# Three key pieces instead of four in a retention scan, and five changes of order, in a hybrid encoder block

## The chip, the core and the metric

The kernel runs on one core of one Trainium2 chip. The metric is device time in microseconds (us) of one execution. The engines are named as in the profile: PE (TensorE, matmuls) with PEld (its weight loads), DVE (VectorE), ACT (ScalarE), POOL (GpSimd) and SP (SyncE, which here only issues DMAs).

## The reference

One encoder block over 16 learned meta tokens and 1024 positions, width 1024. From one normed input `u` and one wide projection come two branches, which are gated and merged:

```
u = rms_norm(h); z = u @ w_in                     # rq rk rv rg | aq ak av ag | gr ga
# branch A, retention: 4 heads, keys of 128, values of 256, chunks of 128, forward and backward
s     = (q k^T) * decay;  inner = s v             # inside a chunk
kv    = (k * k_decay)^T v                         # a chunk's contribution
state = chunk_decay * state + kv                  # scanned over the chunks
o_r   = inner + (q * q_decay) @ state_prev        # both directions are added
o_r   = group_norm(o_r) * ret_nw * silu(rg);  y_r = o_r @ w_rb
# branch B, windowed attention: 8 heads in 2 groups, +-128 positions, meta keys, sink logit
p     = softmax(rotary(aq) rotary(ak)^T * scale + band)
o_a   = (p @ av) * silu(ag);  y_a = o_a @ w_ab
out   = (sigmoid(gr) * y_r + sigmoid(ga) * y_a) @ w_out
return (h + rms_norm(out))[meta tokens dropped]
```

The queries and keys of both branches are rotated (rotary positions) before use.

## The kernel before

Every float32 product is made of three matmuls (`mm3`): each operand is split into a high part (a cast, on ACT or POOL) and a low part (the rest, `dve_lo` on DVE), and high·high, low·high and high·low are added up in a PSUM bank. So each operand of TensorE comes from a cast on one engine and a subtraction on DVE.

The work goes through these stages, on one timeline without gaps:

1. *Head 0's queries and keys* (about 0 to 28 us), while the input arrives. `outs` holds one PSUM bank for each piece of columns; `evac_qk0` rotates the pieces later, three DVE operations and a POOL addition each.
2. *The retention* of four heads (to about 325 us). `retention(h, fill, begin)` scans the chunks c = 0..8 forward (`stage1`: value projection, transposed keys, scores; `stage2`: outputs and state), then c = 8..1 backward, where it normalizes and stores. In the backward loop it calls `fill(n)`, which takes n steps from a generator of other work: `gen_qk(h + 1)`, which projects the next head's keys and queries, then some steps of `pre` (partial products of the gates). A step is one `mm3`, so a piece of columns has KT = 8 steps whatever its width. `KEYS` does not exist here: keys are projected in the four `PIECES` (272, 256, 256 and 256 columns), queries in the two `HALVES` (512 each). `rope_late` rotates a projected piece: two DVE products out of PSUM, and then two accumulating DMAs from POOL's queue, which add the swapped halves. The keys of a head lie in a tile of four parts of 272 columns, `kt`; `ksl(c)` picks a chunk's 128 columns. At the end of the backward scan `begin` starts the next head: its value weights are loaded and split, high part on POOL, low part on DVE.
3. *The attention* (about 330 to 550 us). `gen_av` projects the values; `stage1` (scores `ps`, softmax in `raw`, `p` and `den`), `stage2` (transposes `pt`, their high parts `pah`, `pbh` and low parts `pal`, `pbl`) and `stage3` (`po`) run over 32 chunks, with `fill` in between, its shares in `FILL`. `hooked` counts the filling steps and calls what `BEGUN` lists for a step: `split_q` (high part `aqh`, low part `aql` of rotated queries), `keys(g, i)` (high part `kTh`, low part `kTl` of piece i of the keys of group g), `half_w`, `sum_fetch` and others.
4. *The phases z, r, a and o* (about 545 us to the end): gates, the two branch projections and the output projection, each by seven products per unit instead of eight (`Phase`, `PROD`). `prepare` builds and splits the left operands (`lhz`/`llz` in phase z, `lla` in phase a, `llo` in phase o) up to `LEAD` = 6 products ahead, and leaves the low part that it made last in `ahead[0]`. `refill` loads and splits the right operands of the next phase (`big<-...`, `T<-...`), spread over the products of the phase that runs. Units 0 and 1 of phase z are `early`: they make the sum S4 in three DVE operations at once.

The program's order on each engine is laid out by a planner with a simulated timeline (line 1706), from the order in which the code asks for things and from what it expects each to wait for. `tc.issue_after(i)`, and `follow(...)`, which enters several of them, let an instruction be laid out only after instruction i. Each engine then works through its own list in order.

Of the kernel before, what the change touches and what calls it, by code (L numbers as in the profile page):

```python
# [10 lines left out]
ALU = mybir.AluOpType  # L11
# [8 lines left out]
NH = 4  # L20
EPS = 1e-6
SCALE = 128 ** -0.5
PIECES = [(0, 272), (272, 528), (528, 784), (784, 1040)]
HALVES = [(16, 528), (528, 1040)]
MW = 416
# [14 lines left out]
def block_kernel(ctx: ExitStack, tc: tile.TileContext, x0, xT, x, meta, w_in, w_rb, w_ab, w_out, post_w,  # L40
# [136 lines left out]
    cr = ra.tile([P, T], F32, name="cr")  # L177
    sr = ra.tile([P, T], F32, name="sr")

    held = []  # L180
    BEHIND = "aq1_10", "aq3_10"

    def rope_late(t, a, b, o, nm):

        n = b - a
        m = ra.tile([P, 512], F32, tag="m", bufs=4, name=f"m_{nm}")
        nc.vector.tensor_tensor(m[:, 0:n], t[:, 0:n], sr[:, a:b], ALU.mult)
        nc.vector.tensor_tensor(o[:, 0:n], t[:, 0:n], cr[:, a:b], ALU.mult)

        def rotate():  # L190
            for r in (0, 64):
                nc.gpsimd.dma_start(o[64 - r:128 - r, 0:n], m[r:r + 64, 0:n], accum_op=ALU.add)
        if nm in BEHIND:
            held.append(rotate)
        else:
            rotate()

    def rope_evac(t, a, b, o, nm):
        n = b - a
        m1, m2 = (ra.tile([P, 512], F32, tag="m", bufs=4, name=f"m{i}_{nm}") for i in (1, 2))  # L200
        nc.vector.tensor_tensor(m1[:, 0:n], t[:, 0:n], cr[:, a:b], ALU.mult)
        nc.vector.tensor_tensor(m2[64:128, 0:n], t[0:64, 0:n], sr[0:64, a:b], ALU.mult)
        rot = nc.vector.tensor_tensor(m2[0:64, 0:n], t[64:128, 0:n], sr[64:128, a:b], ALU.mult).ins
        nc.gpsimd.tensor_tensor(o[:, 0:n], m1[:, 0:n], m2[:, 0:n], ALU.add)
        return rot


# [53 lines left out]
    def evac_qk0(*pieces):  # L261
        if 0 not in qk:
            qk[0] = [], ra.tile([P, 4, 272], F32, tag="kp", bufs=2, name="kr0")
        q, kt = qk[0]
        for i in pieces:
            m0, a, b, t = (outs[2:] + outs[:2])[i]
            if m0:
                o = kt[:, i]
            else:
                o = ra.tile([P, 512], F32, tag="q", bufs=6, name=f"qr0_{i}")  # L270
                q.append(o)
            rot = rope_evac(t, a, b, o, f"qk0_{i}")
        return rot

    with tc.tile_pool(name="setup", bufs=1, reuse_waits="tile") as st:
# [46 lines left out]
            nc.tensor.matmul(idle[:, 0:KT * (32 + NM)], zeros[:, 0:P], zeros, start=True, stop=True)  # L322


        outs = [(P, a, b, t(f"pk0_{a}")) for (a, b), t in zip(PIECES, (pj, pj, p1, p3))]
        outs = [(0, a, b, p2(f"pq0_{a}")) for a, b in HALVES] + outs

        def qk0_mm(k):
# [53 lines left out]
        first = [projT(wv0, 0, "pv0_0", vmeta0), projT(wv0, 1, "pv0_1"), projT(wv0, 2, "pv0_2")]  # L382
    ra.tile([P, 32], F32, name="space_q")
    with tc.issue_after(rotated):
        turned = evac_qk0(4)
    with tc.issue_after(turned):
        nc.vector.memset(ms, 1.0)
        nc.vector.tensor_scalar(ms[0:NM, 0:1], sumsq[0:NM, 0:1], 1.0 / D, EPS, op0=ALU.mult, op1=ALU.add)
# [61 lines left out]
    def gen_qk(h):  # L450
        w = load_w(w_in, U_QK + h)
        q, kt = [], ra.tile([P, 4, 272], F32, tag="kp", bufs=2, name=f"kr{h}")
        qk[h] = (q, kt)
        for i, (a, b) in enumerate(PIECES):
            t = yield from proj(w, P, a, b, f"pk{h}_{i}")
            rope_late(t, a, b, kt[:, i], f"k{h}_{i}")
            yield
        for i, (a, b) in enumerate(HALVES):
            t = yield from proj(w, 0, a, b, f"pq{h}_{i}")
            o = ra.tile([P, 512], F32, tag="q", bufs=6, name=f"qr{h}_{i}")  # L460
            rope_late(t, a, b, o, f"q{h}_{i}")
            q.append(o)
            yield
# [3 lines left out]
    def retention(h, fill, begin=lambda: None):  # L467
# [147 lines left out]
        for c in range(NB, 0, -1):  # L615
            o = op[c - 1]
            if c > 1:
                nxt = kvb[c - 1]
                if c < NB:
                    nxt = rp.tile([P, 256], F32, tag="S", bufs=2, name=f"Sb{h}_{c}")  # L620
                    nc.vector.scalar_tensor_tensor(nxt, state["b"], cdb(h), kvb[c - 1], op0=ALU.mult, op1=ALU.add)
                state["b"] = nxt
                state["bs", c - 1] = split_state(nxt, f"b{h}_{c}")
            if c < NB:
                bh, bl = state["bs", c]
                pb = p3(f"pb{h}_{c}")
                last["pb"] = mm3(pb[:, 0:256], qs(qh, c), qs(ql, c), bh, bl, True, True)
                nc.vector.scalar_tensor_tensor(o, pb[:, 0:256], qdb(h, c), o, op0=ALU.mult, op1=ALU.add)
            bs = rp.tile([P, 6], F32, tag="bs", bufs=2, name=f"bs{h}_{c}")
            mv = rp.tile([P, 2], F32, tag="mv", bufs=2, name=f"mv{h}_{c}")  # L630
            rs = rp.tile([P, 1], F32, tag="rs", bufs=2, name=f"rs{h}_{c}")
            nc.vector.bn_stats(bs, o)
            nc.vector.bn_aggr(mv, bs)
            near = nc.vector.tensor_scalar(rs, mv[:, 1:2], EPS, None, op0=ALU.add).ins
            nc.gpsimd.tensor_tensor(rs, rs, mhalf[:, 0:1], ALU.pow)
            state["n", c] = lambda o=o, mv=mv, rs=rs: nc.vector.tensor_scalar(o, o, mv[:, 0:1], rs, op0=ALU.subtract,
                                                                              op1=ALU.mult)
            if c < NB:
                with tc.issue_after(near):
                    state["n", c + 1]()  # L640
            if c < 8:
                with ExitStack() as behind:
                    for p in pins:
                        behind.enter_context(tc.issue_after(p))
                    fill(KT)
            if c == 1:
                begin()
            if c < NB - 1:
                finish(c + 2)
# [20 lines left out]
    def split_q(hp, e_, i):  # L670
# [4 lines left out]
            if len(aqs) == 1:  # L675
                aw.tile([P, 48], F32, name="space_aq")
        h, l = (t.rearrange("p (t e q) -> p t e q", e=2, q=64)[:, :, e_] for t in aqs[hp, i][0])
        nc.scalar.copy(h, o)
        dve_lo(l, o, h)
        aqs[hp, i][1].add(e_)  # L680


    def fetch_aq(hp):
# [47 lines left out]
    def gen_ak(g, pieces_=range(4)):  # L731
        if not wak:
            wak.append(load_w(w_in, U_AK))
        for i in pieces_:
            a, b = PIECES[i]
            t = yield from proj(wak[0], P * g, a, b, f"pak{g}_{i}")
            o = rotated_k[g, i] = ra.tile([P, 272], F32, tag="ak", bufs=2, name=f"akr{g}_{i}")
            rope_late(t, a, b, o, f"ak{g}_{i}")
            if not g and i:
                keys(g, i - 1)  # L740
            yield
# [133 lines left out]
    with tc.issue_after(normed):  # L875
        evac_qk0(2)
        decay_table((0,))
        evac_qk0(3, 5)
    heads, drains = [], []

    def begin_head(h):
# [21 lines left out]
    def gen_av():  # L903
        w = load_w(w_in, U_AV)
        for c in range(9):
            mt = None if c else vmt
            t = projT(w, c, f"pav{c}", mt)
            if c == 0:
# [5 lines left out]
                for r in range(2):  # L914
                    nc.sync.dma_start(vm[32 * r + NM:32 * r + 2 * NM].bitcast(F32), mt)
            else:
                nc.scalar.activation(vah[:, c - 1], t[:, 0:256], AF.Copy, scale=rcol[:, c:c + 1])
                nc.vector.scalar_tensor_tensor(low_value(c - 1), t[:, 0:256], rcol[:, c:c + 1],
                                               vah[:, c - 1].bitcast(F32), op0=ALU.mult, op1=ALU.subtract)
# [46 lines left out]
    class Phase:  # L966
# [24 lines left out]
        def prepare(self, u, p):  # L991
# [30 lines left out]
                    g(t, self.block(u, "A12"), t, sub)  # L1022
            elif u in self.early:
                t = lp.tile([P, 4, P], F32, tag="st", bufs=3, name=f"st{self.nm}{u}S4")
                g(t, self.block(u, "A21"), self.block(u, "A22"), add)
                g(t, t, self.block(u, "A11"), sub)
                g(t, self.block(u, "A12"), t, sub)
                self.split(u, 3, t)
# [125 lines left out]
    def refill(nm, src):  # L1154
# [24 lines left out]
            for k, j in enumerate(n):  # L1179
                at.setdefault(j, []).append(lambda k=k: f(k))  # L1180

        if nm == "a":
            at = {-16: [load(0, 0)], -14: [load(1, 1)]}
            each(at, -13, split("B11", 0, 0))
            at.update({-11: [got("T1")], -10: [load(1, 0)], -9: [got("T2")], -5: [got("T3")], -1: [got("T4")]})
            each(at, -7, split("B21", 1, 0))
            each(at, -3, split("B22", 1, 1))
            return at

        first = -21 if nm == "z" else -17  # L1190
        at = {first: [load(0, 0), load(0, 1)], -13: [load(1, 1)], -9: [load(1, 0, range(3))]}
        def behind(f):
            def g(k):
                with tc.issue_after(ahead[0]):
                    f(k)
            return g

        step(at, range(first + 2, first + 6), behind(minus((0, 1), (0, 1), (0, 0))))
        step(at, (-13, -12, -11, -10), split("B11", 0, 0))
        step(at, (-11, -10, -9, -8), split("T1", 0, 1))  # L1200
# [209 lines left out]
    def attention():  # L1410
# [123 lines left out]
                 gen_aq(3, 0), gen_aq(3, 1), pre]  # L1534
        fill = filler([hooked(works, BEGUN)])[0]

        with follow(*latest):
            fill(3)
        with follow(*latest):
            stage1(0, 0)  # L1540
        for k, (hp, n) in enumerate(chunks):
# [28 lines left out]
            if k in (12, 14, 21):  # L1570
# [13 lines left out]
             76: [(sum_row, 3, 1)], 79: [(sum_fetch, 4)], 82: [(split_q, 2, 0, 0)], 88: [(sum_row, 4, 0)],  # L1584
             89: [(sum_row, 4, 1)], 90: [(split_q, 2, 1, 0)], 92: [(sum_fetch, 5)], 100: [(sum_row, 5, 0)],
             101: [(sum_row, 5, 1)], 102: [(fetch_aq, 3)], 104: [(keys, 1, 1)], 105: [(sum_fetch, 6)],
             110: [(split_q, 2, 0, 1)], 116: [(keys, 1, 2)], 117: [(half_w, 'q', 3, 0)], 121: [(half_w, 'q', 3, 1)],
             122: [(pre_fetch, 9)], 123: [(sum_row, 6, 0)], 124: [(sum_row, 6, 1)], 126: [(split_q, 2, 1, 1)],
             127: [(sum_fetch, 7)], 133: [(pre_sum, 9, 0)], 134: [(pre_sum, 9, 1)], 136: [(keys, 1, 3)],
             139: [(pre_sum, 9, 2)], 140: [(pre_parts, 9)], 141: [(pre_fetch, 10)], 145: [(split_q, 3, 0, 0)],  # L1590
             146: [(sum_row, 7, 0)], 147: [(sum_row, 7, 1)], 150: [(split_q, 3, 1, 0)], 152: [(pre_sum, 10, 0)],
             153: [(pre_sum, 10, 1)], 155: [(pre_sum, 10, 2)], 157: [(pre_parts, 10)], 158: [(pre_fetch, 11)],
             164: [(split_q, 3, 0, 1)], 166: [(pre_sum, 11, 0)], 167: [(pre_sum, 11, 1)], 168: [(pre_sum, 11, 2)],
             170: [(pre_parts, 11)], 171: [(pre_fetch, 12)], 172: [(split_q, 3, 1, 1)], 176: [(pre_sum, 12, 0)],
             178: [(pre_sum, 12, 1)], 179: [(pre_sum, 12, 2)], 181: [(pre_parts, 12)], 182: [(pre_fetch, 13)],
             187: [(pre_sum, 13, 0)], 188: [(pre_sum, 13, 1)], 189: [(pre_sum, 13, 2)], 190: [(pre_parts, 13)]}

# [112 lines left out]
```

## Time and profile before

| | us |
|---|---|
| median of 3 timed runs | 1034.35 |
| lowest and highest | 1034.12, 1037.31 |
| the profiled execution, whole | 1035.83 |
| the profiled execution, its span | 1034.1 |

| engine | busy us | share of the span | instructions |
|---|---|---|---|
| PE | 1022.3 | 99% | 5883 |
| PEld | 898.8 | 87% | 5883 |
| DVE | 831.9 | 80% | 1802 |
| ACT | 502.0 | 49% | 1129 |
| POOL | 226.3 | 22% | 368 |

A span runs from the first to the last instruction of the profiled execution; the execution's own time is 1.73 us longer. In rows of the timeline the columns are start and duration in us, engine, line of the code, operation, what it writes `<-` what it reads (buffer numbers left out), shape, count, and in brackets the engine's idle time just before and what ended it. Rows of the view of waits give who waited for what, the total in us, how often, and the longest.

### The profile page before, as it was taken

The numbers are of one execution on the slowest core, as the hardware profiler recorded it, in microseconds if no ns is written. First come the engines' busy times: TensorE is split into PE (matmuls) and PEld (weight loads), VectorE is DVE, ScalarE is ACT, GpSimd is POOL, SyncE is SP. The second block draws the span as 40 slices with busy tenths as digits, with TensorE's granted clock in tenths as the row PEclk, the third lists the DMA queues.
The fourth block names the chain that finished last, engine by engine and source line by source line (L and its number), as shares of the span: only waits on it lengthen the run. The fifth ranks groups of instructions, "written<-read, shape, count | busy, mean of one in ns | idle before, by whom it ended". The sixth has DMA issues, their size and how long they took to land. (4 is left out here: it accounts for less than half of the span.)

```text
span 1034.1 us, 17322 instructions
## 1 busy us (share of the span) xinstructions
PE 1022.3 (99%) x5883; PEld 898.8 (87%) x5883; DVE 831.9 (80%) x1802; ACT 502.0 (49%) x1129; POOL 226.3 (22%) x368
## 2 busy tenths in 40 slices
PE   9999999999999999999999999999999999999997
PEld 8998999989989888988888888888888888887886
DVE  7886759758876787777769999998989899777765
ACT  5531432523423466655667555455567456333442
POOL 3445244243341424443310000000000000110032
PEclk9999999999999999999999999999999999999999
DMA  9433123243241447666559589899874756889563
GB/s 360 164 87 88 63 46 87 76 78 112 80 97 62 103 152 206 184 183 174 154 171 347 178 287 330 312 319 319 276 265 141 257 196 200 246 216 330 139 122 81
DMA packets 98840, 188.45 MB, mean 182 GB/s; under 512 B 13024, under 2 KB 37632, under 8 KB 98192
## 3 DMA queue, kind: packets, MB, share of 16 engines
q1 hardware_dynamic: 81200, 162.89, 46.6%
q0 software_dynamic: 10176, 14.73, 9.5%
q10 hardware_dynamic: 7376, 9.73, 2.8%
q8 instruction: 46, 0.75, 0.3%
q14 instruction: 42, 0.34, 0.1%
HBM read 124.32 MB, written 57.68 MB: 176 GB/s over the span
## 5 line engine op out<-in xcount | busy, mean ns | idle before, releaser
L1310 POOL DMA_DIRECT2D mx_d<-c1a x4 | 3.6, 891 | 395.3 <-DMA a<-in_w_out_dram 368.6
L77 PE MATMUL bz<-big,llz 128*128 128x512 f32 x192 | 74.9, 390 | 0.5 <-DVE llz L92 0.5
L78 PE MATMUL bz<-big,lhz 128*128 128x512 f32 x192 | 74.4, 389 | 0.0
L76 PE MATMUL bz<-big,lhz 128*128 128x512 f32 x192 | 74.1, 389 | 0.0
L76 PE MATMUL pv<-wh,big 128*128 128x256 f32 x256 | 72.9, 285 | 0.0
L77 PE MATMUL pv<-wh,big 128*128 128x256 f32 x256 | 72.8, 284 | 0.0
L78 PE MATMUL pv<-wl,big 128*128 128x256 f32 x256 | 72.7, 284 | 0.0
L78 PE MATMUL bz<-T,lhz 128*128 128x512 f32 x176 | 68.5, 389 | 0.0
L77 PE MATMUL bz<-T,llz 128*128 128x512 f32 x176 | 68.5, 389 | 0.0
L76 PE MATMUL bz<-T,lhz 128*128 128x512 f32 x176 | 68.2, 389 | 0.0
L1450 ACT ACTIVATE p<-raw,nm 128x337 f32<-128x337 f32 (+1 forms) x64 | 35.5, 557 | 34.1 <-DVE nm L1447 30.5
L76 PE MATMUL paq<-big,wh 128*128 128x512 f32 x128 | 51.6, 403 | 0.0
L1463 POOL TENSOR_SCALAR p<-p,den 128x336 f32<-128x336 f32 (+2 forms) x60 | 32.6, 565 | 85.9 <-DVE den L1454 81.1
L78 PE MATMUL paq<-big,wh 128*128 128x512 f32 x128 | 50.2, 392 | 0.0
L77 PE MATMUL paq<-big,wl 128*128 128x512 f32 x128 | 50.2, 392 | 0.0
L76 PEld LDWEIGHTS pv<-wh,big 128*128 128x128 f32 x256 | 48.4, 189 | 0.4
L77 PEld LDWEIGHTS pv<-wh,big 128*128 128x128 f32 x256 | 48.3, 189 | 0.4
L78 PEld LDWEIGHTS pv<-wl,big 128*128 128x128 f32 x256 | 48.3, 189 | 0.3
L92 DVE TENSOR_TENSOR wl<-wr,wh 128x1024 fp32r<-128x1024 f32 x28 | 35.1, 1258 | 11.3 <-POOL wh L89 6.7
L77 PEld LDWEIGHTS bz<-big,llz 128*128 128x128 f32 x192 | 36.1, 188 | 8.1 <-DVE llz L92 0.8
L78 PEld LDWEIGHTS bz<-big,lhz 128*128 128x128 f32 x192 | 36.0, 188 | 7.5
L76 PEld LDWEIGHTS bz<-big,lhz 128*128 128x128 f32 x192 | 36.1, 188 | 7.5
(621 smaller groups left out, 3591.2 us busy)
## 6 DMA issues: line engine op xcount, KB each, us to landing
wrz<-in_w_in_dram SPq DMA_DIRECT2D x32, 512.0 KB, 6.0
wr<-in_w_in_dram SPq DMA_DIRECT2D x29, 512.0 KB, 4.0
we<-in_w_in_dram SPq DMA_DIRECT2D x16, 512.0 KB, 4.2
tg<-tg_d SPq DMA_DIRECT2D x32, 256.0 KB, 5.3
e<-e ACTq DMA_DIRECT2D x20, 256.0 KB, 2.4
e<-e SPq DMA_DIRECT2D x20, 256.0 KB, 4.6
xn<-in_x_dram SPq DMA_DIRECT2D x8, 512.0 KB, 9.4
oTr_d<-ost SPq DMA_DIRECT2D x16, 256.0 KB, 2.1
```

What stands on the lines that cost most here:

```text
L76: nc.tensor.matmul(o, ah, bh, start=first, stop=False, **kw)
L77: nc.tensor.matmul(o, al, bh, start=False, stop=False, **kw)
L78: latest[:] = [nc.tensor.matmul(o, ah, bl, start=False, stop=last, **kw).ins]
L92: return nc.vector.tensor_tensor(o, i, hi.bitcast(F32), ALU.subtract).ins
L1310: nc.gpsimd.dma_start(d, to, accum_op=ALU.add)
L1450: last["exp"] = nc.scalar.activation(pp[:, x_, w0 - o:w0 - o + 1 + wid], r[:, 0:1 + wid], AF.Exp, scale=-1.0, bias=nm_[:, x_:x_ + 1], accu ...
L1463: nc.gpsimd.tensor_scalar(v, v, den[:, x_:x_ + 1], 1.0, op0=ALU.mult, op1=ALU.mult)
```

## The change

The retention's keys are projected in three pieces, `KEYS`, of 272, 256 and 512 columns. The last one is written through a view of two parts of 256 columns in `kt` (`key_piece`, and `like` for the operands beside it). The shares in the backward scans of heads 0 to 2 become 9, 5, 6, 6, 6, 8, 8 steps for c = 1..7, 48 in all, instead of 8 each; for head 3 they stay at 8. Head 0's pieces are evacuated accordingly, one fewer, and the last key piece takes the bank of tag `p3`.

Five changes of order stand beside that:

- `gen_av` stops once more after the last value projection and before its evacuation; the attention first splits both queries of pair 0 and lays that evacuation out behind their casts (`split_q` returns its cast for that);
- `keys(1, 2)` moves from filling step 116 to 120;
- `split_q(3, 1, 1)` moves from filling step 172 to 169;
- the first sum of S4 of the early units is laid out behind `ahead[0]`;
- in `refill`, the splits of the output projection's right operands (phase "a") are laid out behind `ahead[0]`, as those of other phases were.

```diff
+KEYS = [(0, 272), (272, 528), (528, 1040)]
 PIECES = [(0, 272), (272, 528), (528, 784), (784, 1040)]
...
+    def key_piece(t, i, n):
+        return t[:, 2:4, 0:256] if i == 2 else t[:, i, 0:n]
+
+    def like(t, o):
+        return t.rearrange("p (a c) -> p a c", a=2) if len(o.shape) > 2 else t
...
-        nc.vector.tensor_tensor(o[:, 0:n], t[:, 0:n], cr[:, a:b], ALU.mult)
+        nc.vector.tensor_tensor(o, like(t[:, 0:n], o), like(cr[:, a:b], o), ALU.mult)
...
-                nc.gpsimd.dma_start(o[64 - r:128 - r, 0:n], m[r:r + 64, 0:n], accum_op=ALU.add)
+                nc.gpsimd.dma_start(o[64 - r:128 - r], like(m[r:r + 64, 0:n], o), accum_op=ALU.add)
...
-        outs = [(P, a, b, t(f"pk0_{a}")) for (a, b), t in zip(PIECES, (pj, pj, p1, p3))]
+        outs = [(P, a, b, t(f"pk0_{a}")) for (a, b), t in zip(KEYS, (pj, p1, p3))]
...
-        turned = evac_qk0(4)
+        turned = evac_qk0(3)
...
-        for i, (a, b) in enumerate(PIECES):
+        for i, (a, b) in enumerate(KEYS):
             t = yield from proj(w, P, a, b, f"pk{h}_{i}")
-            rope_late(t, a, b, kt[:, i], f"k{h}_{i}")
+            rope_late(t, a, b, key_piece(kt, i, b - a), f"k{h}_{i}")
...
-                    fill(KT)
+                    fill(KT if h == NH - 1 else (9, 5, 6, 6, 6, 8, 8)[c - 1])
...
-        nc.scalar.copy(h, o)
+        upper = nc.scalar.copy(h, o).ins
         dve_lo(l, o, h)
         aqs[hp, i][1].add(e_)
+        return upper
...
         evac_qk0(2)
         decay_table((0,))
-        evac_qk0(3, 5)
+        evac_qk0(4)
...
             else:
+                if c == NB:
+                    yield
                 nc.scalar.activation(vah[:, c - 1], t[:, 0:256], AF.Copy, scale=rcol[:, c:c + 1])
...
                 t = lp.tile([P, 4, P], F32, tag="st", bufs=3, name=f"st{self.nm}{u}S4")
-                g(t, self.block(u, "A21"), self.block(u, "A22"), add)
+                with tc.issue_after(ahead[0]):
+                    g(t, self.block(u, "A21"), self.block(u, "A22"), add)
...
+        def behind(f):
+            def g(k):
+                with tc.issue_after(ahead[0]):
+                    f(k)
+            return g
+
         if nm == "a":
             at = {-16: [load(0, 0)], -14: [load(1, 1)]}
-            each(at, -13, split("B11", 0, 0))
+            each(at, -13, behind(split("B11", 0, 0)))
             at.update({-11: [got("T1")], -10: [load(1, 0)], -9: [got("T2")], -5: [got("T3")], -1: [got("T4")]})
-            each(at, -7, split("B21", 1, 0))
-            each(at, -3, split("B22", 1, 1))
+            each(at, -7, behind(split("B21", 1, 0)))
+            each(at, -3, behind(split("B22", 1, 1)))
             return at
...
+        with follow(*[split_q(0, e_, 0) for e_ in range(2)]):
+            next(av, None)
         with follow(*latest):
             fill(3)
...
-             110: [(split_q, 2, 0, 1)], 116: [(keys, 1, 2)], 117: [(half_w, 'q', 3, 0)], 121: [(half_w, 'q', 3, 1)],
+             110: [(split_q, 2, 0, 1)], 117: [(half_w, 'q', 3, 0)], 120: [(keys, 1, 2)], 121: [(half_w, 'q', 3, 1)],
...
-             170: [(pre_parts, 11)], 171: [(pre_fetch, 12)], 172: [(split_q, 3, 1, 1)], 176: [(pre_sum, 12, 0)],
+             169: [(split_q, 3, 1, 1)],
+             170: [(pre_parts, 11)], 171: [(pre_fetch, 12)], 176: [(pre_sum, 12, 0)],
```

More of the change, by code (lines that the diff above doesn't have):

```diff
@@ L203, in rope_evac @@
         rot = nc.vector.tensor_tensor(m2[0:64, 0:n], t[64:128, 0:n], sr[64:128, a:b], ALU.mult).ins
[L204 removed]
+        nc.gpsimd.tensor_tensor(o, like(m1[:, 0:n], o), like(m2[:, 0:n], o), ALU.add)
         return rot
@@ L267, in evac_qk0 @@
             if m0:
-                o = kt[:, i]
+                o = key_piece(kt, i, b - a)
             else:
@@ L737, in gen_ak @@
             o = rotated_k[g, i] = ra.tile([P, 272], F32, tag="ak", bufs=2, name=f"akr{g}_{i}")
-            rope_late(t, a, b, o, f"ak{g}_{i}")
+            rope_late(t, a, b, o[:, 0:b - a], f"ak{g}_{i}")
             if not g and i:
@@ L1196, in behind @@
             return g
+        if nm == "a":
+            at = {-16: [load(0, 0)], -14: [load(1, 1)]}
+            each(at, -13, behind(split("B11", 0, 0)))
+            at.update({-11: [got("T1")], -10: [load(1, 0)], -9: [got("T2")], -5: [got("T3")], -1: [got("T4")]})
+            each(at, -7, behind(split("B21", 1, 0)))
+            each(at, -3, behind(split("B22", 1, 1)))
+            return at
+        first = -21 if nm == "z" else -17
+        at = {first: [load(0, 0), load(0, 1)], -13: [load(1, 1)], -9: [load(1, 0, range(3))]}
         step(at, range(first + 2, first + 6), behind(minus((0, 1), (0, 1), (0, 0))))
```

6 lines of the change are left out of this document (removed).

## The prediction

> **What bounds the kernel now.** I read the view of cores first, then the page's busy times, then the waits of TensorE alone, then the stretches of the timeline around each of those waits.
>
> ```profile
> core 0: 1034.1 us, clock 0.998
> ```
> ```profile
> PE 1022.3 (99%) x5883; PEld 898.8 (87%) x5883; DVE 831.9 (80%) x1802; ACT 502.0 (49%) x1129; POOL 226.3 (22%) x368
> ```
> ```profile
> PE idle L322 <- DVE warm L216: 1.4, 1, 1.4
> PE ps L77 <- DVE aql L92: 1.0, 2, 0.5
> PE ba L76 <- DVE u3a L1077: 0.6, 1, 0.6
> PE pt L1483 <- DVE pal L92: 0.5, 1, 0.5
> PE bz L77 <- DVE llz L92: 0.5, 1, 0.5
> PE pt L1487 <- DVE pbl L92: 0.4, 1, 0.4
> ```
>
> TensorE (PE) runs at the full granted clock (0.998) and is busy for 1022.3 of 1034.1 us. So the time moves only by what TensorE itself has to do, or by what it waits for. The list of its waits is short, and apart from the one at the very start every line in it names a VectorE (DVE) result. One more fact is needed to read the sizes: a matmul's row lasts longer than the step to the next one (0.39 us against 0.23 for 512 columns), because matmuls are pipelined. The idle time in a row's bracket therefore understates the loss by about 0.16 us.
>
> The profiled execution took 1035.83 us, its span plus 1.73; the median of the three timed runs is 1034.35, which is 1.48 lower. I work out a difference against the profiled execution and apply it to the median. About 0.3% (3.1 us) is what a measurement of this kernel can tell from no change, so below 1031.25 counts as faster.
>
> **The keys in three pieces.** The projections of the retention's keys change from 272, 256, 256, 256 columns to 272, 256, 512. Each piece is 8 steps of 3 matmuls, so per head 48 matmuls of 256 columns become 24 of 512: 96 such pairs over four heads. The steps come from the timeline of head 1's projections (first and last matmul of a run of 12 with 256 columns, and of 15 with 512):
>
> ```profile
> 72.86 0.28 PE L76 MATMUL pk<-big,wh 128*128 128x256 f32 x1
> ...
> 74.16 0.28 PE L78 MATMUL pk<-big,wh 128*128 128x256 f32 x1
> ```
> ```profile
> 76.67 0.39 PE L76 MATMUL pq<-big,wh 128*128 128x512 f32 x1
> ...
> 79.87 0.39 PE L78 MATMUL pq<-big,wh 128*128 128x512 f32 x1
> ```
>
> 1.30 / 11 = 0.118 us against 3.20 / 14 = 0.2286 us: a pair costs 0.2364, its successor 0.2286, so 0.0078 is saved, 0.7 us over 96. Rounding of the rows leaves about 0.002 a pair, so the saving is 0.5 to 0.9 us; I take 0.6. [...] What else the piece changes lies beside TensorE: each head has one evacuation fewer on VectorE and one pair of rotating DMAs fewer on GpSimd's queue, while the remaining evacuation is a longer block. VectorE has 20% of idle time in all and GpSimd 78%, so I count that at nothing; if the longer block delays something, it shows as a new wait, below.
>
> **The five changes of order.** Each of them stands where TensorE waits, so each is costed by that wait and by what would be late next.
>
> *Attention's first queries* (`split_q(0, ...)` ahead of the last value's evacuation).
>
> ```profile
> 332.70 0.39 PE L77 MATMUL ps<-kTh,aql 128*128 128x272 f32 x1 [0.51 <-DVE aql L92]
> ```
> ```profile
> 329.92 0.47 ACT L917 ACTIVATE vah<-pav,rcol 128x256 fp32r<-128x256 f32 x1 [1.68 <-PE pav L78]
> 330.30 1.13 ACT L678 CAST aqh<-aq 128x512 fp32r<-128x512 f32 x2
> ```
>
> TensorE loses 0.51 + 0.16 = 0.67. ScalarE (ACT) stood idle for 1.68 us for the last value projection, and the casts of the queries, which name no wait of their own, came behind it. Put first, they can start 330.30 − 328.24 = 2.1 us earlier and the low parts on VectorE behind them: all of the 0.67 goes. The evacuation that is put behind them still starts when its projection ends (329.9), and its result is first used some chunks later. −0.67.
>
> *The third keys piece of group 1* (`keys(1, 2)` from step 116 to 120).
>
> ```profile
> 457.30 0.71 PE L1483 MATMUL pt<-ident,p 128*128 128x128 f32 x4 [0.47 <-DVE pal L92]
> 458.44 0.41 PE L1487 MATMUL pt<-ident,p 128*128 128x128 f32 x2 [0.42 <-DVE pbl L92]
> ```
> ```profile
> 452.43 0.42 DVE L92 TENSOR_TENSOR kTl<-akr,kTh 128x256 fp32r<-128x256 f32 x1 [0.88 <-ACT kTh L724]
> ...
> 456.47 0.69 DVE L92 TENSOR_TENSOR pal<-pt,pah 128x512 fp32r<-128x512 f32 x1 [0.30 <-ACT pah L1493]
> ```
>
> VectorE idles 0.88 behind a key piece that isn't there yet, works 0.42 on it, and the scores (`raw`), the exponentials, `pah` and `pal` follow in one chain to the two transposes. Taken out of this place, 1.3 us come off the chain; the waits are 0.47 + 0.16 and 0.42 + 0.15, together 1.2. All of it should go, −1.2, as long as the piece's new place, four filling steps on, lies after the next scores. Two POOL rows show what an ill meeting costs there: the same scaling of two weight tiles took 1.07 us in one chunk and 1.82 in the next.
>
> ```profile
> 456.34 1.07 POOL L1463 TENSOR_SCALAR p<-p,den 128x336 f32<-128x336 f32 x2 [0.21 <-DVE den L1454]
> ...
> 463.45 1.82 POOL L1463 TENSOR_SCALAR p<-p,den 128x336 f32<-128x336 f32 x2
> ```
>
> [...]
>
> *The last queries* (`split_q(3, 1, 1)` from step 172 to 169).
>
> ```profile
> 516.85 0.42 PE L77 MATMUL ps<-kTh,aql 128*128 128x336 f32 x1 [0.53 <-DVE aql L92]
> ```
>
> Loss 0.53 + 0.16 = 0.69. Three steps earlier is one chunk earlier (the shares of pair 3 are five steps, and 172 opens one), at least 5 x 3 x 0.2286 = 3.4 us of TensorE's filling; the low part then costs its 0.68 us of VectorE in a chunk where it stands ahead of nothing that was late. −0.69.
>
> *The gates' first sums* (S4 of the units 0 and 1 behind the last split).
>
> ```profile
> 546.39 0.50 PE L77 MATMUL bz<-big,llz 128*128 128x512 f32 x1 [0.45 <-DVE llz L92]
> ```
> ```profile
> 544.32 0.69 DVE L1025 TENSOR_TENSOR stz0S<-wrz,wrz 128x512 f32<-128x512 f32 x1 [3.66 <-DMA wrz<-in_w_in_dram]
> 545.04 0.69 DVE L1026 TENSOR_TENSOR stz0S<-stz0S,wrz 128x512 f32<-128x512 f32 x1
> 545.65 0.68 DVE L92 TENSOR_TENSOR llz<-wrz,lhz 128x512 fp32r<-128x512 f32 x1
> ...
> 554.82 0.68 DVE L92 TENSOR_TENSOR llz<-stz1S,lhz 128x512 fp32r<-128x512 f32 x1
> ```
>
> Loss 0.45 + 0.16 = 0.61. Two sums stand ahead of the low part that the first product needs. Without them it could start about 0.5 us earlier, when its high part is cast. But the sums have to be done all the same: from 544.32 on no row of VectorE up to the last one quoted has idle time before it, and the low part of the fourth product ends at 555.50, where TensorE, three products of 12 x 0.2286 = 2.74 us and an attention remnant later, asks for it. VectorE's wait for the cast can come back there. Between 0 and −0.61; I take −0.4.
>
> *The output projection's right side* (its splits behind the last left split).
>
> ```profile
> 942.52 0.51 PE L76 MATMUL ba<-big,lha 128*128 128x512 f32 x1 [0.56 <-DVE u3a L1077]
> ```
> ```profile
> 935.76 0.69 DVE L1009 TENSOR_TENSOR sto1S<-wro 128x512 f32<-128x512 f32 x1 [4.18 <-DMA wro<-mx_d]
> ...
> 937.58 1.89 DVE L92 TENSOR_TENSOR big<-a,big 128x512 fp32r<-128x512 f32 x3
> ...
> 941.79 0.68 DVE L1077 TENSOR_TENSOR u3a<-u3a,ba 128x512 f32<-128x512 f32 x1
> ```
>
> Loss 0.56 + 0.16 = 0.72. VectorE is blocked 4.18 us by a DMA and then has a backlog, in which splits for a later phase (`big<-a`, about 0.6 each) come ahead of the sum that TensorE waits for. One split moved behind it gives 0.6, two give all; but the changed order holds the splits only behind `lla`, not behind `u3a`, and may move nothing. Between 0 and −0.72; I take −0.4.
>
> **New waits.** The program's order comes from a planner, so every stretch behind the first edit is laid out anew. The rows show one-off waits of 0.4 to 0.7 us each; I allow for up to three new ones, 0 to +1.8, and take +0.4.
>
> **Sum.** −0.6 − 0.67 − 1.2 − 0.69 − 0.4 − 0.4 + 0.4 = −3.56: 1032.3 for the profiled execution and 1030.8 for the median. With every term at its best end (−0.9 − 0.67 − 1.2 − 0.69 − 0.61 − 0.72) it is −4.8, 1029.6; with the two doubtful terms at nothing and one more wait of 0.6 it is −2.2, 1032.2.
>
> **The rivals.** *The waits move on* (0.19): VectorE's queue, not the order within it, is what is late. Then the gates' wait comes back at the fourth product, `u3a` stays where it is, and half of the 1.2 at the transposes stays with the `pbl` that follows. Left are −0.6 − 0.67 − 0.69 − 0.6 and +0.6 of new waits: −2.0, 1032.4. For it speaks that VectorE has no gap after 544.32; against it, that the first three terms are waits behind work that wasn't ready, not behind a full queue.
>
> *Slower: the next head's second half of the value weights comes late* (0.12).
>
> ```profile
> 89.34 1.21 POOL L89 TENSOR_SCALAR wh<-wr 128x1024 fp32r<-128x1024 f32 x1 [1.49 <-PE pq L78]
> ```
> ```profile
> 91.49 1.21 DVE L92 TENSOR_TENSOR wl<-wr,wh 128x1024 fp32r<-128x1024 f32 x1
> ```
>
> GpSimd gets that buffer when the projection of the second queries half lets go of it, and the weights are ready at 92.70, 3.4 us later. Today what follows in the fill covers this. The new shares put the end of that projection into the last share, beside the steps of the early gate sums. If the planner then runs those steps before it, TensorE has only half a value projection (8 x 0.118 = 0.9 us) as cover and loses up to 2.4 us at each of three head boundaries: +7.2 − 3.6 = +3.6, 1038.0. It decides above 1.2 us a boundary. Against it: the steps leave the generator in a fixed order, and no boundary waits now.
>
> *The order doesn't change on the chip* (0.03): the planner already placed the constrained instructions there. Then the keys alone are left, −0.6, 1033.8.
>
> **How the numbers follow.** My forecast, with 0.66, is 1030.8, its own range 1029.4 to 1032.2; about 0.04 of it lies above 1031.25. Of the moved waits 0.03 come out below that bound, the rest within 0.3%. So faster 0.62 + 0.03 = 0.65; same 0.04 + 0.16 + 0.03 = 0.23; slower 0.12. For the range I go from 1029.0 (every term at its best, with 0.6 for the spread of runs) to 1033.6, which takes in the moved waits; outside are the slower rival and a few hundredths at either end.
>
> **What the changed profile would show.** Right: 72 fewer matmuls in the three later heads and 24 fewer in head 0 (5883 to about 5787), `pk` with 512 columns at 0.23 us a step, no `ps <- aql`, no `bz <- llz` and no `ba <- u3a` in the list of TensorE's waits, and `raw` ahead of `kTl` in its chunk. Wrong: a wait of the value projections (`pv`) on `wl` at a head boundary, a wait of `bz` near the fourth product, new lines above 0.5 us in that list, or `raw` still behind a key piece.

## The result, and the profile after

The changed kernel took 1048.88 us (median of 4 runs, 1047.82 to 1050.04) beside 1035.05 for the kernel before (4 runs): a ratio of 1.013, 95% interval 1.0113 to 1.0147. The prediction, 1030.8 with faster as the likeliest, was wrong: the change costs 13.8 us.

The view of cores, the page's busy times and the head of the list of TensorE's waits (total, times, longest), all of the changed kernel:

```profile
core 0: 1046.7 us, clock 0.995
```
```profile
PE 1029.4 (98%) x5787; PEld 896.4 (86%) x5787; DVE 832.6 (80%) x1793; ACT 502.2 (48%) x1129; POOL 224.4 (21%) x361
```
```profile
PE bz L77 <- ACT lhz L997: 3.2, 1, 3.2
PE idle L329 <- DVE warm L223: 1.4, 1, 1.4
PE bz L78 <- DVE llz L93: 0.8, 1, 0.8
PE pe L78 <- DVE wel L93: 0.8, 1, 0.8
PE to L611 <- ACT ost L616: 0.6, 1, 0.6
PE to L611 <- DVE op L643: 0.5, 2, 0.3
```

The matmuls are 96 fewer, as they should be, but a new wait of 3.2 us for `lhz` heads the list, waits of the scan stand in it (`to`), and the mean clock is lower (0.995 instead of 0.998). To see the whole loss, which a row's bracket understates (3.20 us for the wait at 563.91, where the step from the matmul before, at 560.33, is 3.58 instead of 0.23), I took the starts of consecutive matmuls and counted what a step exceeds the median step of matmuls with as many columns. Regular steps add up to 1014.9 us before and 1014.3 after. What exceeds them (us), by stage of the work:

| kernel | start | scan | attention | gates' start | phases to 920 us | o phase | sum |
|---|---|---|---|---|---|---|---|
| before | 2.3 | 1.7 | 5.4 | 0.9 | -0.5 | 0.8 | 10.5 |
| after | 2.3 | 7.3 | 5.7 | 8.8 | -0.5 | 0.3 | 23.8 |

So the loss has two places: the scan (about 100 to 335 us), +5.6, and the first products of the gates (about 550 to 580 us), +7.9. The later tables go by the same stages. Their stage columns come from the one profiled execution of each kernel, which can lie some 3 us from the kernel's median (that of `keys_alone` took 1042.55 us, its median is 1039.48); so they show where a kernel waits, and the medians what it costs. At the gates, the rows of TensorE, VectorE and ScalarE of the changed kernel and the stretches around them (length, then busy time of PE, PEld, DVE, ACT, POOL, the granted clock, DMA):

```profile
563.91 1.58 PE L77 MATMUL bz<-big,lhz 128*128 128x512 f32 x3 [3.20 <-ACT lhz L997]
566.34 0.79 PE L78 MATMUL bz<-big,llz 128*128 128x512 f32 x1 [0.85 <-DVE llz L93]
```
```profile
550.47 0.69 DVE L93 TENSOR_TENSOR llz<-wrz,lhz 128x512 fp32r<-128x512 f32 x1 [4.50 <-ACT lhz L997]
...
552.40 0.69 DVE L93 TENSOR_TENSOR llz<-wrz,lhz 128x512 fp32r<-128x512 f32 x1
553.01 0.68 DVE L1036 TENSOR_TENSOR stz0S<-wrz,wrz 128x512 f32<-128x512 f32 x1
...
555.79 0.69 DVE L93 TENSOR_TENSOR big<-xT,big 128x512 fp32r<-128x512 f32 x1 [0.64 <-ACT big L973]
557.16 0.69 DVE L93 TENSOR_TENSOR llz<-stz0S,lhz 128x512 fp32r<-128x512 f32 x1 [0.68 <-ACT lhz L997]
557.77 0.69 DVE L1036 TENSOR_TENSOR stz1S<-wrz,wrz 128x512 f32<-128x512 f32 x1
...
561.98 0.69 DVE L1038 TENSOR_TENSOR stz1S<-wrz,stz1S 128x512 f32<-128x512 f32 x1
562.58 3.10 DVE L93 TENSOR_TENSOR T<-xT,T 128x512 fp32r<-128x512 f32 x5
565.59 0.69 DVE L93 TENSOR_TENSOR llz<-stz1S,lhz 128x512 fp32r<-128x512 f32 x1
```
```profile
561.16 2.18 ACT L973 CAST T<-xT 128x512 fp32r<-128x512 f32 x4 [0.50 <-DMA xT<-xs]
563.25 0.61 ACT L997 CAST lhz<-stz1S 128x512 fp32r<-128x512 f32 x1
```
```profile
558.00:565.00 7.00, 3.76 (x14) 2.31 (x14) 7.00 (x13) 5.63 (x12) 0.00 (x0) 1.00 1.06 397
565.00:572.00 7.00, 6.15 (x14) 4.60 (x15) 7.00 (x13) 5.09 (x10) 0.00 (x0) 0.52 0.93 334
572.00:579.00 7.00, 7.00 (x32) 5.76 (x31) 6.97 (x13) 1.98 (x4) 0.00 (x0) 0.99 0.40 118
```

Before, two of unit 0's S4 sums ran ahead of the first low part, in part in time in which VectorE would have waited for that low part's cast: without them it idles 4.50 us there, instead of 3.66 ahead of the first sum. Now none starts before 553.01. Unit 1's three sums stand behind the low part of unit 0's product, with five other operations between the first and the last, and end at 562.67; TensorE has been waiting since 560.7. Counted from the first cast (544.51 before, 549.81 after), that end comes 9.2 us later before the change and 12.9 after it. Of these 3.7 us, 0.84 are the longer wait ahead of the first low part, 0.64 and 0.68 the two waits for casts in the rows above, where before unit 1's sums filled the time, and 1.2 are two splits of T1 more that now come ahead. Then the splits of T2 and T4, due much later, stand ahead of the high part's cast and for 3.1 us ahead of the low part (565.59), where the second wait comes from. And the clock is at half (0.52) from 565 to 572: the clock's records put it at 565.29 to 572.11, 6.83 us. A step of 512 columns takes 0.43 us there instead of 0.23; the steps behind the second wait lose about 2.8 us by it.

### The profile page after: what moved, and what is told of

It reads as the page before. It is cut to its first block, busy times and chain, and to the rows that moved or that the text cites. A ratio compares the mean times of both kernels' runs of the same rounds, so it can differ in the third digit from the quotient of the medians.

```text
span 1046.7 us, 17132 instructions
## 1 busy us (share of the span) xinstructions
PE 1029.4 (98%) x5787; PEld 896.4 (86%) x5787; DVE 832.6 (80%) x1793; ACT 502.2 (48%) x1129; POOL 224.4 (21%) x361
## 5 line engine op out<-in xcount | busy, mean ns | idle before, releaser
L77 PE MATMUL bz<-big,lhz 128*128 128x512 f32 x192 | 75.7, 396 | 3.2 <-ACT lhz L997 3.2
L79 PE MATMUL bz<-big,lhz 128*128 128x512 f32 x192 | 75.1, 394 | 0.0
L616 ACT ACTIVATE ost<-to,rnw 128x128 f32<-128x128 f32 x64 | 19.9, 365 | 49.8 <-PE to L611 43.3
```

Source lines behind the costliest of these rows:

```text
L77: nc.tensor.matmul(o, ah, bh, start=first, stop=False, **kw)
L79: latest[:] = [nc.tensor.matmul(o, ah, bl, start=False, stop=last, **kw).ins]
L616: nc.scalar.activation(ost[0][:, e_, w0:w0 + P], to[:, P * e_:P * e_ + P], AF.Copy, scale=rnw[:, 2 * h + e_:2 * h + e_ + 1])
```

## The experiments

### Which part costs

`s4_alone` and `no_s4` have the edit on the S4 sums alone, and all but it:

```
+                with tc.issue_after(ahead[0]):
                     g(t, self.block(u, "A21"), self.block(u, "A22"), add)
```


> The kernel before with one edit alone: the S4 sums of the gates' units 0 and 1 behind the low part split last. Theory (the gates' first sums cost the time): the second unit's sums start only behind the low part of the product before, TensorE stands some 3.4 us before its fourth product and the clock is at half for some 7 us behind it; +7 to +10 us against the kernel before, 1042 to 1045. Rival (the scan, laid out anew for the keys, costs the time): no new wait there of over 1 us; -0.5 to +1, about 1035.

> The changed kernel without that one edit (S4 sums where they were). Theory: 8 to 13 us come back, 1036 to 1041, the clock is whole around the first products of the gates. Rival: the time stays within 2 us of the changed kernel's, 1047 to 1049.

`five_orders` has the five changes of order and the old keys, `keys_alone` the new keys and shares and the old orders:

> The kernel before with all five changes of order and the keys left in four pieces. Theory: the gates' stall of +9 and the four other waits of -0.7, -1.2, -0.7, -0.4 at the most: +6 to +9, 1041 to 1044. Rival (the keys and their shares cost the time): 1031 to 1034, as the prediction had it for the orders.

> The kernel before with the keys in three pieces and the new shares alone. Theory: -0.7 for the matmuls and about +3 of new short waits between 100 and 375 us: +1 to +4, 1036 to 1039, and no half clock at the gates. Rival (the keys make most of the loss): +8 to +14, 1043 to 1049. The prediction's own term: -0.6, 1034.4.

| kernel | median us | ratio to before, interval | scan | gates' start |
|---|---|---|---|---|
| `s4_alone` | 1042.99 | 1.0066 (1.0046 to 1.0087) | 1.4 | 8.5 |
| `no_s4` | 1041.12 | 1.0050 (1.0035 to 1.0065) | 7.3 | 0.7 |
| `five_orders` | 1045.24 | 1.0086 (1.0069 to 1.0103) | 1.4 | 8.9 |
| `keys_alone` | 1039.48 | 1.0038 (1.0026 to 1.0049) | 7.3 | 1.6 |

The two places belong to two edits: the gates' loss comes with the S4 edit and only with it (`s4_alone` costs 7.0 us), the scan's with the keys and only with them (`keys_alone` costs 3.5). The rival, that the keys make most of it, falls. `no_s4`, `five_orders` and `keys_alone` lie 0.1 to 1.2 us above the ranges expected by the theory.

### The four other orders

> The kernel before with four changes of order (attention's first queries, third keys piece, last queries, right side of the output projection), without the gates' sums and with the keys as before. The prediction's terms: -0.7 -1.2 -0.7 -0.4, 1032 to 1033. What five_orders against s4_alone points to: they cost 1 to 2, 1037 to 1038, in new waits of TensorE on weight splits around 515 to 530 us and on the output projection at 950 us.

1036.23 beside 1035.74, ratio 1.0004 (0.9995 to 1.0013): no change, where the prediction's terms made -3.0. So each by itself:

> The kernel before with attention's first queries alone put ahead of the last value's evacuation. The prediction's term: -0.7, 1035.0 beside 1035.7, the wait at 332 us gone. If what four_orders showed as no change came from this edit bringing waits elsewhere: 1036 or more.

> The kernel before with the last queries alone moved from step 172 to 169. The prediction's term: -0.7, the wait on the low part of the queries at 516 us gone. What four_orders points to: that wait goes and two on the weights' split of an early gate sum come at 525 us, 0.5 and 1.0 us, so +0.5 to +1, 1036.2 to 1036.7.

> The kernel before with the splits of the output projection's right side alone behind the last left split. The prediction's term: -0.4 (0 to -0.72), the wait at 942 us shorter. What the combinations point to (that wait was between 0 and 1.0 us without this edit and between 0 and 1.2 with it): no change, 1035.5 to 1036.3.

*First queries* (`a_alone`): 1035.20 beside 1035.93, 0.9992 (0.9983 to 1.0), and the wait at 332 us is gone, as forecast. It is the only version whose median lies below that of the kernel before, though by hardly more than can be measured: the interval reaches to no change. *Last queries* (`e_alone`): 1.0005 (0.9994 to 1.0016). Its list of TensorE's waits has no wait of this chunk on `aql`, but

```profile
PE pe L77 <- DVE wel L92: 1.3, 2, 0.8
```

The low part of the queries, 0.68 us, now stands ahead of the weights' split of an early gate sum (`wel` starts at 513.03, 0.52 later than before), which was no wait before: 0.50 us at 514.31. The second, 0.77 at 527.02, comes behind a cast of ScalarE that `wel` waits for; why that is late stays open. The attention stage exceeds by 6.5 instead of 5.4. *Right side* (`c_alone`): 1.0005 (0.9994 to 1.0016). The wait on `u3a` varies between profiled executions without the edit from 0 (`s4_alone`) over 0.56 (before) to 0.7 (`keys_alone`), and with it from 0 (`c_alone`) over 0.34 (`four_orders`) to 1.0 (`no_s4`); no effect can be told from that. *Third keys piece*: the program with this edit alone has the same order on all four engines as the kernel before, instruction for instruction, so it was not timed. In `four_orders` the piece stands where it stood, with a longer wait ahead of it than the 0.88 before:

```profile
452.53 0.43 DVE L92 TENSOR_TENSOR kTl<-akr,kTh 128x256 fp32r<-128x256 f32 x1 [1.96 <-ACT kTh L725]
```

### Why the S4 sums cost so much

`t_splits_later` is the changed kernel with the splits of T2 to T4 behind the fourth product's (the cut below); `s4_first_unit_only` has the S4 order for unit 0 alone; `s4_clear` lays the splits of T1 and the S1 sums behind the fourth product's split as well.

```
-            split_b(n, k, t)                                   # get_sum
+            with follow(hi_of["z", 1, 3], lo_of["z", 1, 3]) if n != "T1" else ExitStack():
+                split_b(n, k, t)
```


> The changed kernel with the splits of the combined activations T2 to T4 laid behind the split of the fourth product's left operand, on ScalarE and on VectorE; the S4 sums stay behind the low part. If those splits ahead of the cast and of the low part make the stall: it falls from 3.4 + 2.4 us to under 1, and with it the half clock; 1039 to 1042. If the sums themselves come too late on VectorE (the third of them ends at 562.7, TensorE asks at 560.6): about 3 us of stall stay, the 2.4 behind it go, 1043 to 1046, less 3 more if the clock then stays whole.

> The changed kernel with the order on the S4 sums for unit 0 alone; unit 1's are free again. Theory (it is unit 1's sums, which wait for the low part of unit 0's own, that come too late): the stall before the fourth product falls under 1.5 us and the clock stays whole, 1040 to 1043, near no_s4. Rival (unit 0's delayed sums push the whole queue of VectorE): stall over 2.5 us, 1045 to 1049.

> The changed kernel, its order on the S4 sums kept, and what VectorE and ScalarE had between them laid behind the fourth product's split: the S1 sums of units 0 and 1 and all splits of T1 to T4. If it is the place in the queue (the sums of unit 1 alternate with five other operations of 0.6 us each and end at 562.7, TensorE asks at 560.6): unit 1's sums end about 3 us earlier, the stall and the half clock go, about 1040 to 1041. If the sums themselves are too much for VectorE between the third and the fourth product: a stall of over 1.5 us stays, 1044 to 1048.

| kernel | median us | ratio, interval | gates' start | phases to 920 us |
|---|---|---|---|---|
| `t_splits_later` | 1047.97 | 1.0126 (1.0109 to 1.0143) | 6.6 | 1.2 |
| `s4_first_unit_only` | 1047.59 | 1.0121 (1.0104 to 1.0137) | 4.8 | 0.3 |
| `s4_clear` | 1051.83 | 1.0147 (1.0131 to 1.0163) | 2.0 | 8.2 |

All three expectations of a recovery failed. Without the T splits the second wait went, but the first stayed at 2.63, since the sums still ended at 563.3. With unit 1 free, its sums alternate with unit 0's, and the third product's operand came late by 1.56. And `s4_clear` took the stall away where it was (unit 1's sums end at 559.7) and found it again 14 us on:

```profile
578.23 0.50 PE L77 MATMUL bz<-T,lhz 128*128 128x512 f32 x1 [3.40 <-ACT lhz L998]
```

That points to a debt of VectorE in the whole stage rather than to one bad place. Two rows of stretches, before and `s4_alone`, show it (DVE is the third busy time):

```profile
550.00:555.00 5.00, 5.00 (x24) 4.14 (x24) 5.00 (x10) 4.22 (x9) 0.00 (x0) 1.00 1.06 396
```
```profile
550.00:555.00 5.00, 4.78 (x21) 3.51 (x20) 3.50 (x6) 3.20 (x7) 0.00 (x0) 1.00 1.06 404
```

Before, VectorE is busy for all of these 5 us and for the 5 after. In `s4_alone` it idles 1.5 of them, waiting for two casts, and two sums (1.3 us) that ran ahead of the first low part before come behind it. Two runs were to tell the bound from the order:

```
-                g(t, self.block(u, "A21"), self.block(u, "A22"), add)
+                for _ in range(3 if u == 0 else 1):            # delay2
+                    g(t, self.block(u, "A21"), self.block(u, "A22"), add)
```
```
-        dve_lo(l, as_(src), h)                                 # s4_gps, a_gps, for T1 to T4
+        nc.gpsimd.tensor_tensor(l, as_(src), h.bitcast(F32), ALU.subtract)
```


> The kernel before with the first S4 sum of unit 0 computed three times over (two more sums of 0.65 us on VectorE, nothing else; the splits of T2 to T4 stay behind the fourth product's). If VectorE is the bound in this stage: each sum is paid by TensorE, 1.2 to 1.4 us of new waits before the third and fourth products, 1037.0 to 1037.5, or 2 more if the clock falls. If it has slack and only the order counts: no new wait over 0.3, 1035.5 to 1036.2.

> s4_alone (1043.0) with the low parts of the splits of T1 to T4 on GpSimd instead of VectorE. If VectorE is the bound: unit 1's sums stand one behind the other and end about 2.4 us earlier, a stall of under 1 us is left before the fourth product, the clock stays whole; 1036 to 1038. If the order behind the low part alone costs (each of the two units' sums, casts and low parts in a chain): the stall stays over 2.5 us, 1041 to 1043.

`delay2`: 1040.38, 1.0048 (1.0029 to 1.0066). Two sums of 0.6 us each on VectorE, and TensorE waits at the third product where it had not:

```profile
554.26 0.50 PE L77 MATMUL bz<-big,llz 128*128 128x512 f32 x1 [1.32 <-DVE llz L92]
```

The 1.2 us put in come out as a wait of 1.3, as they would if VectorE is the bound in this stage. The run does not separate load from order, though: the planner also moved unit 0's last S4 sum from 546.26 to 550.51, behind other work. (The stage exceeds by 2.5 instead of 0.9, as forecast; the whole kernel costs 4.9 us, more than either expectation, since further waits of 4.3 us in all lie at 638 to 796 us. How they follow stays open.) `s4_gps` came out at 1050.37, 1.0147 (1.0128 to 1.0166), far from both expectations. With the low parts on GpSimd, VectorE's sums beside them took 1.78 us instead of 0.69:

```profile
552.09 1.78 DVE L1029 TENSOR_TENSOR stz1S<-wrz,wrz 128x512 f32<-128x512 f32 x1
```
```profile
552.02 4.67 POOL L965 TENSOR_TENSOR big<-xT,big 128x512 fp32r<-128x512 f32 x3 [0.40 <-ACT big L963]
```

So it is no test of the bound. The version that was to profit from it did not either:

> The kernel before with attention's first queries put ahead (a_alone, 1035.2) and the low parts of the splits of T1 to T4 on GpSimd, the S4 sums where they were. If VectorE is the bound at the gates' start: the wait of 0.6 at 545 us stays, as it lies ahead of those splits, but others behind it go: 1034.5 to 1035.3. If GpSimd is slower at it than the products ask: new waits on T1 or T2, 1036 or more.

1045.41, 1.0099 (1.0083 to 1.0115): the gates' start exceeds by only 1.4, but GpSimd works for 13.6 us on the splits from 561.7 on, VectorE's operations beside it take up to 1.78, and TensorE waits 4.3 us at 578 for an evacuation (`u2z`) that stands in ScalarE's queue behind such an operation; the phases after the gates' start exceed by 10.6.

### What of the keys costs

```
-                    fill(KT if h == NH - 1 else (9, 5, 6, 6, 6, 8, 8)[c - 1])
+                    fill(KT)                                   # keys_old_shares
```
```
+                for j in (0, 256):                             # half_evac, last piece of the later heads
+                    rope_late(t[:, j:j + 256], a + j, a + j + 256, kt[:, 2 + j // 256, 0:256], ...)
```


> The kernel before with the keys in three pieces, but the scan's shares left at eight steps each (against keys_alone, which came out at 1039.5 beside 1036.0 for the kernel before). If the new shares make the new waits at the heads' ends: those of about 120, 126, 190, 326 and 331 us go, 1034 to 1036. If the pieces themselves do (the long last piece holds VectorE or GpSimd): they stay, 1038 to 1040.

> The kernel before with the keys in three pieces on TensorE (as keys_alone), but for the three later heads the last piece is evacuated and rotated as two of 256. If the longer evacuation delays the scan: the waits at about 120, 126, 190, 326 and 331 us go, 1034 to 1036. If the projection's longer steps shift the scan's chain (its forward pass ends 5 to 8 us later with three pieces): they stay, 1038.5 to 1040.

`keys_h0` and `keys_later` have three pieces in head 0 alone, and in the three later heads alone:

> The kernel before with the keys in three pieces in head 0 alone. If head 0's longer piece delays its scan's forward pass and so all that follow: the waits at 120 and 126 us stay and those at 190 with them, +1.5 to +2.5, 1037.3 to 1038.3. If the later heads' projections do it by their longer steps: no new wait, 1035.7 to 1036.0.

> The kernel before with the keys in three pieces in the three later heads and four in head 0. If head 0 alone makes the scan late: the waits at 120 and 126 us are gone, 1035.0 to 1036.0, with 0.5 of saved matmul steps. If the later heads' longer pieces cost by themselves: new waits at 190 and 326 to 331 us, 1037 to 1039.

| kernel | median us | ratio, interval | scan | attention |
|---|---|---|---|---|
| `keys_old_shares` | 1039.38 | 1.0042 (1.0027 to 1.0056) | 7.4 | 5.3 |
| `half_evac` | 1037.96 | 1.0020 (1.0010 to 1.0030) | 4.5 | 6.3 |
| `keys_h0` | 1040.16 | 1.0051 (1.0031 to 1.0071) | 3.3 | 6.6 |
| `keys_later` | 1038.74 | 1.0039 (1.0023 to 1.0055) | 7.3 | 5.7 |

The shares do nothing: with the old ones the same waits stand at the same places. The pieces do it: in the scan, those of head 0 alone make 1.9 us, those of the later heads alone 5.9 (against 1.4 in the unchanged scan of `s4_alone`), and both together no more than 5.9. So the two do not add up, nor do the medians: head 0 alone costs 4.7 us, above both expectations, the later heads alone 2.6, both together 3.5. `keys_h0` does not have the waits at 120 and 126 us, which were expected to stay, and why it also loses outside the scan (the attention exceeds by 6.6 instead of 5.4) stays open. Further, evacuating the last piece in halves takes the waits at 326 and 331 us away but leaves those at 120 to 196. What the pieces do to the scan is seen in the last output product `pa` of the forward pass of heads 0 and 1 and in the last `pv` of head 1's value projections, before:

```profile
87.12 0.28 PE L78 MATMUL pa<-Slf,qh 128*128 128x256 f32 x1
...
125.13 0.28 PE L78 MATMUL pv<-wl,big 128*128 128x256 f32 x1
...
153.96 0.28 PE L78 MATMUL pa<-Slf,qh 128*128 128x256 f32 x1
```

and after:

```profile
92.48 0.28 PE L79 MATMUL pa<-Slf,qh 128*128 128x256 f32 x1
...
123.96 0.37 PE L79 MATMUL pv<-wl,big 128*128 128x256 f32 x1
...
162.35 0.28 PE L79 MATMUL pa<-Slf,qh 128*128 128x256 f32 x1
```

The scan, a chain over four engines, runs 5.4 and 8.4 us later, while the projections that cover it end 1.2 us earlier. Where the cover is used up, TensorE waits for the chain, after:

```profile
126.57 0.38 PE L77 MATMUL pkv<-vh,khf 128*128 128x256 f32 x1 [0.40 <-ACT khf L517]
...
331.52 0.44 PE L611 MATMUL to<-ident,op 128*128 128x128 f32 x2 [0.65 <-ACT ost L616]
```

In head 0 the start of the shift can be named. Before, the first scaled keys (`klf`, at 42.67) came ahead of the evacuation of the second half of the queries, 2.1 us of VectorE; with the longer piece that evacuation is laid ahead of them, and they come at 45.37, 2.7 us later:

```profile
42.67 0.33 DVE L511 SCALAR_TENSOR_TENSOR klf<-tr,kdr,khf 16x128 fp32r<-16x128 f32 x1
```
```profile
45.37 0.59 DVE L518 SCALAR_TENSOR_TENSOR klf<-tr,kdr,khf 16x128 fp32r<-16x128 f32 x2
```

Why the later heads shift too is seen only as a new order laid out by the planner; which of its steps decides stays open.

## Why the prediction was wrong

- **The gates' first sums: the step that failed most.** The prediction saw that VectorE has no idle time after 544.32, and that its wait "can come back" at the fourth product, and then bounded the term by 0, as if work put off could at worst cost nothing. In place of a term between 0 and -0.61, the edit alone costs 7.0 us, and TensorE waits 3.2 us at the very product, the fourth, that the prediction named. Three things were left out. The 0.84 us of the sums that ran while VectorE would have waited for a cast were free there, and nowhere later. With unit 1's sums held back, VectorE had nothing to do during two casts and idled (0.64 and 0.68), on an engine without slack. And behind the waits the clock was at half for 6.83 us: about 2.8 of the loss.
- **The keys.** The term for the matmuls was right: regular steps fell by 0.67, forecast 0.6 (0.5 to 0.9). "I count that at nothing" was the error: what the piece changes beside TensorE cost 5.6 us in the scan, where the planner lays out the order anew; the kernel with the keys alone costs 3.5. The allowance for new waits (+0.4, up to 1.8) was made from one-off waits and was too small by three times.
- **The slower rival** had the place (the heads' ends) and nearly the price for this part (7.2 forecast, 5.6 measured), but by luck, as the mechanism was another: where the first waits lie `wl` comes no later (125.50 after, 126.49 before), no wait of TensorE names it, and the waiting matmuls name `khf`, `op` and `ost`, the scan itself.
- **First queries**: the mechanism was right, the queries' wait is gone; -0.7 was forecast, and the medians differ by as much, though the interval (0.9983 to 1.0) reaches to no change.
- **Third keys piece** (-1.2): a step later in the code was taken for a place later in VectorE's queue. The program does not change; the rival "the order doesn't change" was right for this edit.
- **Last queries** (-0.69): the wait went, and two on `wel` came, one of them behind the moved low part. The claim that the low part "stands ahead of nothing that was late" was not checked against the weights' split.
- **Right side** (-0.4): no effect that can be told; the wait it aims at comes and goes by itself between executions.

Together: the four orders make nothing (forecast -3.0), keys and gates +10.5 by themselves and 13.8 with all edits at once. The 3 us between are not explained by any single run. Some of it seems to lie between the S4 edit and the four orders: `five_orders` costs 9.3 us, `s4_alone` 7.0 and `four_orders` 0.5, but the intervals of the first two overlap.

## What to carry to other kernels

Before moving work behind something, look whether it now runs in time in which its engine would wait anyway, and whether that engine has slack for the next ten microseconds; if it has none, a new wait in its queue can be paid in full by the engine that counts (here 1.2 us put in came out as 1.3), and the bound of the term is not zero. Where a planner lays out the program, compare the orders of the two programs before pricing an edit: one of these edits moved nothing, and one that saves 0.7 us of matmuls moved the whole scan. A wait that is taken away on a full queue can show up at a later consumer (here, in `s4_clear`, 14 us on, as 3.40); look for that one first.

## What the runs showed of the hardware

TensorE's clock fell to half behind some of its waits. It stayed there for 3.4 us in `s4_first_unit_only` (behind a wait of 1.56 us and four matmuls in a row of 2.32 us) and in `t_splits_later` (2.63), and for 6.8 us in the changed kernel (3.20), in `s4_alone` (3.42), in `five_orders` (TensorE idle for 3.57 us in all between 553 and 560) and in `s4_gps` (4.24). In `a_gps`, behind 4.31 us, a step of 512 columns takes 0.43 us instead of 0.23 from 579.03 on. The 1.32 us in `delay2` left the clock whole, but so did the 3.40 in `s4_clear`, so it is not the length of the wait alone:

```profile
560.00:565.00 5.00, 4.94 (x11) 3.31 (x12) 5.00 (x9) 5.00 (x10) 0.00 (x0) 0.66 1.06 398
```
```profile
575.00:580.00 5.00, 1.77 (x7) 1.25 (x8) 5.00 (x10) 2.96 (x5) 0.00 (x0) 1.00 0.27 100
```

(the first of `s4_first_unit_only`, behind its wait, the second of `s4_clear`, around its wait.) The clock's records of the changed kernel change at 5.50, 565.29, 572.11 and 1043.15 us, which are 164, 2 and 138 times 3.413 us apart. In the 3.41 us ahead of 565.29 three matmuls started, 0.68 us of regular steps (0.227 each); in the 3.41 ahead of the half clock of `s4_gps` none did. But in `s4_clear` none started for 3.78 us either, from 574.45 to 578.23, and the clock stayed at 1.00. What decides was not shown.

GpSimd's subtractions and VectorE's sums, each with two inputs, took longer beside each other in `s4_gps`: VectorE's sum took 1.78 us instead of 0.69 while GpSimd worked at its own for 1.56 each (4.67 for three), instead of the 1.31 of one that ran just before, beside an almost idle VectorE. The cause was not shown. Idle time of GpSimd was no reserve for these subtractions of VectorE: with them on GpSimd the ratio is 1.0147 (`s4_gps`) instead of 1.0066 (`s4_alone`), and 1.0099 (`a_gps`) instead of 0.9992 (`a_alone`).
